# Three quarters of a down projection by seven block products, and constant products while the first tokens load

## The chip, the cores and the metric

The kernel runs on one core of a Trainium2 chip. Its engines are TensorE (PE, matrix products; PEld is its loading of the stationary operand), VectorE (DVE), ScalarE (ACT), GpSimd (POOL) and SyncE (SP); each works its own queue in order and waits for the others by semaphores. The metric is the time of one execution on the device in microseconds; less is better.

## What is computed

A decoder of two layers over 512 tokens of width 1024: differential attention, then latent attention, each followed by a feed-forward part with a squared ReLU, and a last normalization. The change lies in the feed-forward part of the second layer and at the very start.

```python
def sq_relu_mlp(hn, w_up, w_down):
    return jnp.square(jax.nn.relu(hn @ w_up)) @ w_down
...
            h = h + mla_attention(hn, w_dq[j], q_norm_g[j], w_uq[j], w_o_b[j],
                                  k_nope, k_rope, v, cos_b, sin_b)
        h = h + sq_relu_mlp(rms_norm(h, mlp_norm_g[l]), w_up[l], w_down[l])
    return rms_norm(h, final_norm_g)
```

`w_up` is 1024 x 4096, `w_down` 4096 x 1024, everything in float32.

## The kernel before

Products are made in a type of 32 bits that TensorE takes in one pass (`F32R`). To keep precision each operand is split in a high part (a cast on ScalarE) and a low part (a subtraction on VectorE), and a product is a triple, `mm3` (line 343): high by high, high by low, low by high, each with 128 x 128 stationary and up to 512 moving columns. A k-tile is 128 of the summed dimension, a token tile 128 tokens.

`Weights` (`W`, line 60) streams the weights. A unit of up to 1152 columns is loaded to one of 4 raw buffers (`load`, DMAs on SP's queue), cast (`prep_h`, L101) and subtracted (`prep`, L113) into one of 3 pairs of buffers. `get` takes the next unit, and `ahead` prepares the one behind it while TensorE works on the taken one.

The last feed-forward part goes in two halves of 2048 hidden features. `hidden` (line 672) makes 16 k-tiles of hidden features of all 512 tokens, two per job: 16 triples with the weights stationary and the normalized residual moving. Its `done` takes the ReLU on ScalarE (L676), multiplies it by the product on VectorE (L677: the square), and splits the result (L332, L333). `down_tokens` (line 813) then has the hidden tiles stationary and 512 columns of the down projection moving: for each of the two column halves (`fc`) it sums 16 k-tiles for four token tiles in four PSUM banks, and `token_done` adds them, scaled, to the residual rows `rtok`. Four such passes are made: 4 x 16 x 4 = 256 triples. The last one closes token by token: square and sum on ScalarE, a reciprocal root on GpSimd, two scalings and two output DMAs, whose place in the order of ScalarE's and VectorE's queues is set by due times (`OUT_US`, `later`). `side` (line 215) puts the turning of the residual into token rows (`scale1`) between the triples of the first up projection.

At the start, the identity, the gains and the tokens are loaded. `gain_cols` turns the gains into columns (`gcol`) on TensorE; a DMA that reads `gcol` (`held`) holds back the further loads on SP's queue. Per token tile `turn_x` makes eight transposes, multiplies by the gains on VectorE, splits, and copies the residual; value products fill TensorE between. `sum_x` then squares and sums each token half on ScalarE, and the reciprocal roots follow on GpSimd (`rsqrt_cols`).

A planner fixes the order in each engine's queue when the program is built; it may take an instruction ahead of others written before it, except in stretches in which the written order is kept (`nc.kept`: the start and the last pass).

Of the kernel before, what the change touches and what calls it, by code (L numbers as in the profile page):

```python
# [15 lines left out]
P = 128  # L16
T = 512
# [42 lines left out]
class Weights:  # L60
# [5 lines left out]
    def __init__(self, nc, pool, size):  # L66
        self.nc, self.pool, self.size = nc, pool, size
        self.specs, self.raws, self.parts = [], [], []
        self.taken = self.split = 0
        self.eng = nc.vector  # L70

    def add(self, name, shape, loads, beside=False, outs=None, eng=None):

# [10 lines left out]
    def load(self, upto, queue=None):  # L84
        while len(self.raws) < min(upto, len(self.specs)):
            name, shape, loads, *_ = self.specs[len(self.raws)]
            raw = self.tile(F32, name + "r", "raw", shape, self.RAW)
# [4 lines left out]
    def prep_h(self, upto):  # L92

        while len(self.parts) < min(upto, len(self.specs)):
            n = len(self.parts)
            self.load(n + 1)
            name, shape, _, beside, outs, eng = self.specs[n]
# [6 lines left out]
    def prep(self, upto):  # L104

        self.prep_h(upto)
        while self.split < min(upto, len(self.specs)):
# [8 lines left out]
            self.load(n + 1 + self.RAW)  # L116
# [8 lines left out]
    def ahead(self):  # L125
        self.prep(self.taken + 1)
# [103 lines left out]
OUT_US = (2.3, 2.6)  # L230
ROPE_US = (7, 9.0)
AT_TABLES = 3.5
# [29 lines left out]
def trunk(ctx: ExitStack, tc: tile.TileContext, io: dict, out: bass.AP):  # L262
# [80 lines left out]
    def mm3(dst, a, b, start, stop):  # L343

        (ah, al), (bh, bl) = a, b
        nc.tensor.matmul(dst, ah, bh, start=start, stop=False)  # L346
        nc.tensor.matmul(dst, ah, bl, start=False, stop=False)  # L347
        nc.tensor.matmul(dst, al, bh, start=False, stop=stop)  # L348
# [457 lines left out]
    hid1 = [[], []]  # L806
# [6 lines left out]
    def down_tokens(w_dn, hid, half, fc, last):  # L813

        units = [(w_unit(w_dn, fc * T, T, 16 * half + k, 2, f"m1d{half}{fc}_{k}"), k) for k in range(0, 16, 2)]
        tags = ("s", "s", "tr", "tr") if (half + fc) % 2 else ("acc", "acc", "acc", "o")
        late = 2 if last else 0

        def job():
            dsts = [bank(f"m1d{half}{fc}{i}", t) for i, t in enumerate(tags)]  # L820

            def mul(i, w, k):
                for kk in range(2):
                    yield mm3(dsts[i], sub(hid[k + kk], ALL, slice(i * P, (i + 1) * P)), sub(w, ALL, kk),
                              k + kk == 0, k + kk == 15)

            for u, k in units[:8 - late]:
                w = W.get(u)
                for i in range(NT):
# [3 lines left out]
                    if k == 14:  # L833
                        token_done(i, dsts[i], half, fc)
            ws = [(W.get(u), k) for u, k in units[8 - late:]]
            for i in range(NT if late else 0):
                for w, k in ws:
                    yield from mul(i, w, k)
                token_done(i, dsts[i], half, fc)
        return 16 * NT * 3 * PASS * T, job  # L840

    def token_done(i, dst, half, fc):
        t = rtok[i][fc]
        nc.vector.scalar_tensor_tensor(t, dst, r2c[:, i:i + 1], t, op0=ALU.mult, op1=ALU.add)
        if half == 0:
            return
        junk = big("fjunk")
        nc.scalar.activation(junk, t, AF.Square, accum_out=fss[:, i, fc:fc + 1])
        if fc == 0:
            nc.gpsimd.tensor_mul(t, t, gfin[0][:, :T])  # L850
# [11 lines left out]
        def out_second():  # L862
            nc.vector.scalar_tensor_tensor(t, t, f, gfin[0][:, T:], op0=ALU.mult, op1=ALU.mult)
# [301 lines left out]
```

## Time and profile before

| | us |
|---|---|
| median of 3 runs (lowest, highest) | 1147.07 (1147.04, 1147.47) |
| the profiled execution, its own time | 1147.38 |
| its span, first to last instruction | 1145.6 |
| TensorE busy | 1125.5 (98%) |
| VectorE busy | 649.5 (57%) |
| ScalarE busy | 496.9 (43%) |

A busy share is time in which an instruction of the engine was under way. Ends of matrix products are modelled, and products overlap, so the pace of TensorE is read from the distance of starts. A group is named by its line, the tile it writes and those it reads; L51 stands for all instructions in stretches of kept order, whatever line wrote them. Behind a group's times stands the idle time of its engine just before it, with what ended it.

### The profile page before, as it was taken

To read this page: it belongs to the slowest core of one execution; us is meant where nothing else is said; L and a number is where in the kernel's file an instruction comes from. 1 tells how busy PE (TensorE), PEld (TensorE's weight loads), DVE (VectorE), ACT (ScalarE), POOL (GpSimd) and SP (SyncE) were. 2 spreads that over 40 slices of the span, in tenths; PEclk is the share of its full clock that TensorE was granted. 3 is DMA by queue.
4 is the path that set the end of the run, shared out by engine and by line. 5 is a ranking of instruction groups with operands and counts; after the bars stand their busy time and mean duration, and the time that the engine had idled before them with its cause. 6 is when DMAs were issued, how large, how long until landed. Compare 5 with 4: busy or idle time off the path is not lost.

```text
span 1145.6 us, 14137 instructions
## 1 busy us (share of the span) xinstructions
PE 1125.5 (98%) x5528; PEld 945.5 (83%) x5528; DVE 649.5 (57%) x1148; ACT 496.9 (43%) x910; POOL 70.6 (6%) x63
## 2 busy tenths in 40 slices
PE   7999999999999999999999999999999999999996
PEld 7778998878888888888888889988888888888885
DVE  5898989876443234444455898855444223444232
ACT  6567666654341213443334666534433112343132
POOL 1000000030000010000111000013000000000011
PEclk9999999999999999999999999999999999999998
DMA  7321222123233333332332220123322333333211
GB/s 230 103 71 56 74 75 75 55 74 111 92 94 108 93 92 93 108 94 92 93 100 80 78 74 19 56 92 92 92 92 92 99 103 92 92 101 101 92 55 74
DMA packets 98321, 102.06 MB, mean 89 GB/s; under 512 B 4896, under 2 KB 86478, under 8 KB 98254
## 3 DMA queue, kind: packets, MB, share of 16 engines
q1 hardware_dynamic: 96974, 99.51, 28.2%
q10 hardware_dynamic: 1280, 1.65, 0.4%
q8 instruction: 43, 0.70, 0.2%
q14 instruction: 24, 0.20, 0.1%
HBM read 99.05 MB, written 2.10 MB: 88 GB/s over the span
## 4 chain that ended last, share of the span: by engine, by line
PE 79%; DVE 12%; ACT 4%; issue 2%; DMA 1%; SPq 1%; POOL 1%; ACTq 0%; POOLq 0%; DVEq 0%
PE m0d L346 5%; PE m1u L346 5%; PE m0d L348 5%; PE m1u L348 5%; PE m0u L347 5%; PE m0u L346 5%; PE m0d L347 5%; PE m1u L347 5%; PE m0u L348 5%; PE m1d L347 4%; PE m1d L348 4%; PE m1d L346 4%; PE m1d L51 3%; PE ob L346 1%; PE ob L348 1%
## 5 line engine op out<-in xcount | busy, mean ns | idle before, releaser
L346 PE MATMUL m1u<-xn1h,m1u_4h 128*128 128x512 f32 x128 | 50.3, 393 | 0.0
L346 PE MATMUL m1u<-xn0h,m1u_0h 128*128 128x512 f32 x128 | 50.2, 392 | 0.0
L348 PE MATMUL m1u<-xn1h,m1u_4l 128*128 128x512 f32 x128 | 49.9, 390 | 0.0
L348 PE MATMUL m1u<-xn0h,m1u_0l 128*128 128x512 f32 x128 | 49.9, 390 | 0.0
L347 PE MATMUL m1u<-xn1l,m1u_4h 128*128 128x512 f32 x128 | 49.8, 389 | 0.0
L347 PE MATMUL m1u<-xn0l,m1u_0h 128*128 128x512 f32 x128 | 49.8, 389 | 0.0
L347 PE MATMUL m0u<-xm0l,m0u_0h 128*128 128x512 f32 x128 | 49.8, 389 | 0.0
L346 PE MATMUL m0u<-xm0h,m0u_0h 128*128 128x512 f32 x128 | 49.8, 389 | 0.0
L346 PE MATMUL m0u<-xm1h,m0u_4h 128*128 128x512 f32 x128 | 49.8, 389 | 0.0
L347 PE MATMUL m0u<-xm1l,m0u_4h 128*128 128x512 f32 x128 | 49.8, 389 | 0.0
L348 PE MATMUL m0u<-xm0h,m0u_0l 128*128 128x512 f32 x128 | 49.8, 389 | 0.0
L348 PE MATMUL m0u<-xm1h,m0u_4l 128*128 128x512 f32 x128 | 49.8, 389 | 0.0
L113 DVE TENSOR_TENSOR m1u_4l<-m1u_4r,m1u_4h 128x1024 fp32r<-128x1024 f32 x16 | 19.6, 1225 | 36.5 <-ACT m1u_4h L101 36.5
L113 DVE TENSOR_TENSOR m0u_4l<-m0u_4r,m0u_4h 128x1024 fp32r<-128x1024 f32 x16 | 19.9, 1245 | 33.4 <-ACT m0u_4h L101 33.2
L677 DVE TENSOR_TENSOR m1a<-m1u,m1a 128x512 f32<-128x512 f32 x32 | 22.0, 687 | 21.7 <-ACT m1a L676 21.7
L677 DVE TENSOR_TENSOR m0a<-m0u,m0a 128x512 f32<-128x512 f32 x32 | 21.9, 686 | 19.4 <-ACT m0a L676 19.4
L101 ACT CAST m1u_4h<-m1u_4r 128x1024 fp32r<-128x1024 f32 x16 | 16.8, 1052 | 34.7 <-PE m1u L347 21.6
L676 ACT ACTIVATE m0a<-m0u 128x512 f32<-128x512 f32 x32 | 18.9, 592 | 29.4 <-PE m0u L348 29.4
L676 ACT ACTIVATE m1a<-m1u 128x512 f32<-128x512 f32 x32 | 19.0, 592 | 27.6 <-PE m1u L348 27.6
L101 ACT CAST m0u_4h<-m0u_4r 128x1024 fp32r<-128x1024 f32 x16 | 16.8, 1052 | 31.7 <-PE m0u L347 25.5
L363 POOL TENSOR_TENSOR ssq_m<-ssq_m,sq 128x512 f32<-128x512 f32 x14 | 21.3, 1519 | 149.8 <-ACT sq L362 149.7
L113 DVE TENSOR_TENSOR m0u_0l<-m0u_0r,m0u_0h 128x1024 fp32r<-128x1024 f32 x16 | 21.0, 1310 | 14.7 <-ACT m0u_0h L101 14.4
(2306 smaller groups left out, 3522.9 us busy)
## 6 DMA issues: line engine op xcount, KB each, us to landing
m0u_0r<-in_w_up SPq DMA_DIRECT2D x16, 512.0 KB, 3.7
m0u_4r<-in_w_up SPq DMA_DIRECT2D x16, 512.0 KB, 3.6
m1u_0r<-in_w_up SPq DMA_DIRECT2D x16, 512.0 KB, 3.6
m1u_4r<-in_w_up SPq DMA_DIRECT2D x16, 512.0 KB, 3.7
wq_0r<-in_w_qkv_a SPq DMA_DIRECT2D x8, 512.0 KB, 3.9
wk_0r<-in_w_qkv_a SPq DMA_DIRECT2D x8, 512.0 KB, 5.0
xt<-in_x SPq DMA_DIRECT2D x8, 256.0 KB, 4.8
wv_0r<-in_w_qkv_a SPq DMA_DIRECT2D x4, 512.0 KB, 3.5
```

The lines of the kernel that those rows point to most:

```text
L51: return self.owner.tc.keep_in_program_order(op(*args, **kw))
L101: self.nc.scalar.copy(d(h), v(self.raws[n]))
L113: eng.tensor_sub(d(to), v(self.raws[n]), d(h).bitcast(F32))
L346: nc.tensor.matmul(dst, ah, bh, start=start, stop=False)
L347: nc.tensor.matmul(dst, ah, bl, start=False, stop=False)
L348: nc.tensor.matmul(dst, al, bh, start=False, stop=stop)
L363: eng(nc).tensor_add(accum, accum, sq)
L676: nc.scalar.activation(a, dst, AF.Relu)
L677: nc.vector.tensor_mul(a, dst, a)
```

## The change

Chunks 0 to 2 of 8 k-tiles each (24 of the 32) of the last down projection go by Winograd's form of Strassen's scheme: hidden features A (512 tokens x 1024) and weights B (1024 x 1024) of a chunk are cut in 2 x 2 blocks, and seven products of blocks, or of sums of blocks, take the place of eight. `ORDER` names them with the chain of PSUM banks that each is added to and the quarter of the result that the chain is then added to. The last 8 k-tiles go by `down_tokens`, now with 8 k-tiles in each pass.

The sums of hidden blocks (S1 to S4) and of weight blocks (T1 to T4) are made on VectorE in full precision, and each of the seven operands on either side is then split: `pair` for A, units of `W` for B, with the raw block in place of a load. `hidden_tile` squares on ScalarE, 256 tokens at a time, straight into the A blocks. The up projection of the next chunk is cut in half jobs (4 of the 8 k-tiles for both features) that stand between the block products: product (P), half job (U), and so on, seven of each and an eighth half job. `steps` says what is started with each. `W` is now prepared two units ahead in this stretch. The raw blocks of B lie in buffers of the attention and in the residual's, which has been turned by then.

At the start 18 products of a constant with itself stand ahead of the first transposes and 14 more behind them; the gains are turned behind the first token tile's transposes; `held` reads the identity; four of the eight square sums go to VectorE. At the end the second last token's first scaling has a later due time, and the final gains lie in two tiles.

```diff
...
                 eng.tensor_sub(d(to), v(self.raws[n]), d(h).bitcast(F32))
...
-            self.load(n + 1 + self.RAW)
+            k, ahead = n + 1, 0
+            while k < len(self.specs) and ahead < self.RAW:
+                ahead += not callable(self.specs[k][2])
+                k += 1
+            self.load(k)
...
     def ahead(self):
-        self.prep(self.taken + 1)
+        self.prep(self.taken + self.lead)
...
 SPACE = 0.5
-OUT_US = (2.3, 2.6)
+OUT_US = (2.3, 2.6, 3.0)
 ROPE_US = (7, 9.0)
+WARM = (18, 14)
...
+    class Sevenths:
+        ORDER = (("A11", "B11", "u", [(0, 0)]), ("A12", "B21", "v", [(0, 0)]), ("S2", "T2", "u", [(0, 1)]),
+                 ("S1", "T1", "w", [(1, 1)]), ("S3", "T3", "u", [(1, 1)]), ("S4", "B22", "w", [(0, 1)]),
+                 ("A22", "T4", "u", [(1, 0)]))
+        made = 0
...
+        def hidden_tile(self, n, a):
+            k, u, j = n // 4, n % 4 // 2, n % 2
+            for m in range(2):
+                name = f"A{m + 1}{k + 1}"
+                if j == 0:
+                    self.a.setdefault(name, []).append(big(f"m1{name}{self.at}{u}").rearrange("p (k q) -> p k q", k=2))
+                nc.scalar.activation(self.a[name][u][:, j, :], a[:, m * 256:(m + 1) * 256], AF.Square)
+        def load_b(self, *names):
+            for name in names:
+                k, n = int(name[1]) - 1, int(name[2]) - 1
+                if n == 0:
+                    self.b[name] = [ap.tile([P, 2, T], F32, name=f"m1{name}{self.at}{u}", tag=("ath", "atl")[k], bufs=2)
+                                    for u in range(2)]
+                else:
+                    self.b[name] = [res[:, 4 * k + 2 * u:4 * k + 2 * u + 2, :] for u in range(2)]
+                for u in range(2):
+                    nc.sync.dma_start(self.b[name][u], w_view(self.w_dn, n * T, T, 8 * self.at + 4 * k + 2 * u, 2))
...
+        def sum_a(self, to, x, y, op, place=None):
+            x, y = self.a[x], self.a[y]
+            t = self.a[place] if place else [big(f"m1{to}{self.at}{u}").rearrange("p (k q) -> p k q", k=2) for u in range(2)]
+            for u in range(2):
+                nc.vector.tensor_tensor(t[u], x[u], y[u], op)
+            self.a[to] = t
+        def sum_b(self, to, x, y, place=None):
...
+        def pair(self, name):
+            spare = key_rests[2 * (Sevenths.made % 2):][:2]
+            Sevenths.made += 1
+            self.pairs[name] = [split(a.rearrange("p k q -> p (k q)"), name, tiles=spare[u])
+                                for u, a in enumerate(self.a[name])]
...
+        def product(self, i, units):
+            a, b, chain, to = self.ORDER[i]
+            first = chain not in self.banks
+            if first:
+                self.banks[chain] = [bank(f"m1{chain}{self.at}{t}", "s" if chain == "u" else "tr") for t in range(2)]
+            for u in range(2):
+                w = W.get(units[u])
+                for t in range(2):
+                    for j in range(2):
+                        tok = slice(j * 256 + t * P, j * 256 + (t + 1) * P)
+                        yield mm3(self.banks[chain][t], sub(self.pairs[a][u], ALL, tok), sub(w, ALL, j),
+                                  first and u == j == 0, u == j == 1, skip_group_check=True)
+                        if t == j == 0:
+                            W.ahead()
+                    if u == 1:
+                        for m, n in to:
+                            x = rtok[2 * m + t][n]
+                            tok = 2 * m + t
+                            nc.vector.scalar_tensor_tensor(x, self.banks[chain][t], r2c[:, tok:tok + 1], x,
+                                                           op0=ALU.mult, op1=ALU.add)
...
-        later.add(OUT_US[0], out_first)
+        later.add(OUT_US[2 if i == NT - 2 else 0], out_first)
         later.add(OUT_US[1], out_second)
...
+    CHUNKS = 3
+    sevenths = [Sevenths(c, io["w_down"][1]) for c in range(CHUNKS)]
...
+    def hidden_half(mp, half):
...
+        def done(m, dst):
+            c, n = mp // 4, 2 * (mp % 4) + m
+            a = big("m1a")
+            nc.scalar.activation(a, dst, AF.Relu)
+            if c < CHUNKS:
+                sevenths[c].hidden_tile(n, a)
+            else:
+                nc.vector.tensor_mul(a, dst, a)
+                hid1.append(split(a, "m1h"))
...
+    def seven(c):
...
+        steps = {
+            ("P", 0): lambda: (s.pair("A12"), s.sum_b("T1", "B12", "B11"), s.sum_a("S1", "A21", "A22", ALU.add)),
+            ("U", 0): lambda: (s.sum_b("T2", "B22", "T1"), load("B11")),
+            ("P", 1): lambda: (s.sum_a("S2", "S1", "A11", ALU.subtract), s.pair("S2")),
+            ("U", 1): lambda: s.sum_b("T3", "B22", "B12", "B12"),
+            ("P", 2): lambda: (s.pair("S1"), s.sum_a("S4", "A12", "S2", ALU.subtract, "A12")),
+            ("U", 2): lambda: (s.sum_b("T4", "B21", "T2", "T2"), load("B21")),
+            ("P", 3): lambda: (s.sum_a("S3", "A11", "A21", ALU.subtract, "A21"), s.pair("S3")),
+            ("P", 4): lambda: s.pair("S4"),
+            ("P", 5): lambda: (s.pair("A22"), load("B12")),
+            ("P", 6): lambda: (load("B22"), nxt is not None and nxt.pair("A11")),
+        }
...
+        def job():
+            for i in range(7):
+                yield from with_step(("P", i), s.product(i, plan[i]))
+                yield from with_step(("U", i), halves[i]())
+            yield from halves[7]()
+        return (7 * 8 + 8 * 16 / 2) * 3 * PASS * T, job
+    up1 = [hidden_half(mp, h) for mp in range(4) for h in range(2)]
+    both1 = [seven(c) for c in range(CHUNKS)]
+    down1 = [down_tokens(io["w_down"][1], hid1, fc, fc == 1) for fc in range(2)]
...
-        nc.sync.dma_start(held, gcol[0:1, 0:1])
+        nc.sync.dma_start(held, ident[0:1, 0:1])
...
-    gain_cols(grow_attn, 16, G_ATTN_A)
     more_loads()
+    def warm(n, name):
+        dst = bank(name, "o")
+        for _ in range(n):
+            nc.tensor.matmul(dst[:, :P], ones, ones, start=True, stop=True)
+    warm(WARM[0], "warm0")
...
+        if i == 0:
+            gain_cols(grow_attn, 16, G_ATTN_A)
+            warm(WARM[1], "warm1")
...
-            nc.scalar.activation(junk, xt[i][n], AF.Square, accum_out=ss0[:, 2 * i + n:2 * i + n + 1])
+            ss = ss0[:, 2 * i + n:2 * i + n + 1]
+            if n:
+                nc.vector.tensor_tensor_reduce(junk, xt[i][n], xt[i][n], 1.0, 0.0, ALU.mult, ALU.add, ss)
+            else:
+                nc.scalar.activation(junk, xt[i][n], AF.Square, accum_out=ss)
...
-    side(up1[0], scale1(), 4.0)
-    gfin.append(ap.tile([P, D], F32, name="gfin", tag="atl", bufs=2))
-    nc.sync.dma_start(gfin[0], io["final_norm_g"].rearrange("(o d) -> o d", o=1).broadcast_to([P, D]))
-    Filler(down1[0] + up1[1] + down1[1][:1]).drain()
+    sevenths[0].load_b("B11", "B21")
+    side([(16 * 3 * PASS * T / 2, job) for job in up1[:6]], scale1(), 2.0)
+    sevenths[0].load_b("B12", "B22")
+    sevenths[0].pair("A11")
+    Filler([(16 * 3 * PASS * T / 2, job) for job in up1[6:]]).drain()
+    W.lead = 2
+    Filler(both1).drain()
+    W.lead = 1
+    gfin += [big(f"gfin{n}") for n in range(2)]
+    for n in range(2):
+        nc.sync.dma_start(gfin[n], io["final_norm_g"][n * T:(n + 1) * T].rearrange("(o d) -> o d", o=1).broadcast_to([P, T]))
+    Filler(down1[:1]).drain()
     nc.kept = True
-    Filler(down1[1][1:]).drain()
+    Filler(down1[1:]).drain()
...
```

## Rows read from the trace of the kernel before

**Rows 1.** The page's first part: busy us (share of the span) and instructions.
```profile
PE 1125.5 (98%) x5528; PEld 945.5 (83%) x5528; DVE 649.5 (57%) x1148; ACT 496.9 (43%) x910; POOL 70.6 (6%) x63
```

**Rows 2.** The waits of TensorE: in total us, times, longest; three of eleven.
```profile
PE gps L51 <- DMA grow_attn<-in_attn_norm_g: 4.7, 1, 4.7
PE va0vps L51 <- ACT wv_0h L51: 1.2, 1, 1.2
PE rb_ps L321 <- POOL r L51: 1.1, 1, 1.1
...
```

**Rows 3.** Busy time by stretch: PE, PEld, DVE, ACT, POOL, then clock, DMA share, GB/s.
```profile
60.00:80.00 20.00, 19.25 (x96) 15.63 (x95) 19.76 (x50) 13.87 (x30) 0.00 (x0) 1.00 0.27 79
240.00:260.00 20.00, 20.00 (x90) 16.57 (x89) 17.24 (x18) 12.08 (x18) 10.15 (x7) 1.00 0.35 105
...
910.00:1136.00 226.00, 226.00 (x993) 186.07 (x992) 82.10 (x95) 66.01 (x87) 6.89 (x7) 1.00 0.27 88
```

**Rows 4.** Timeline (start, us, what), the last 72 products: the first and the last.
```profile
1119.63 0.39 PE L51 MATMUL m1d<-m1d_10h,m1hh 128*128 128x512 f32 x1
...
1135.72 0.39 PE L51 MATMUL m1d<-m1d_14h,m1hl 128*128 128x512 f32 x1
```

**Rows 5.** Groups of instructions, 786 to 1136 us: busy us, mean ns, idle before them.
```profile
L677 DVE TENSOR_TENSOR m1a<-m1u,m1a 128x512 f32<-128x512 f32 x32 | 22.0, 687 | 21.7 <-ACT m1a L676 21.7
...
L113 DVE TENSOR_TENSOR m1u_4l<-m1u_4r,m1u_4h 128x1024 fp32r<-128x1024 f32 x15 | 18.4, 1225 | 36.3 <-ACT m1u_4h L101 36.3
...
L333 DVE TENSOR_TENSOR m1hl<-m1a,m1hh 128x512 fp32r<-128x512 f32 x24 | 16.6, 692 | 16.6 <-ACT m1hh L332 16.6
L101 ACT CAST m1u_4h<-m1u_4r 128x1024 fp32r<-128x1024 f32 x15 | 15.8, 1052 | 34.2 <-PE m1u L347 21.6 <-issue 8.2 <-PE m1d L348 4.4
```

**Rows 6.** Timeline of the end.
```profile
1136.35 0.74 DVE L51 SCALAR_TENSOR_TENSOR rt<-m1d,r2c,rt 128x512 f32<-128x512 f32 x1
...
1138.00 0.63 ACT L51 ACTIVATE fjunk<-rt 128x512 f32<-128x512 f32 x1 [0.41 <-ACT rt L51]
```

**Rows 7.** Timeline of the square sums, 24 to 32 us.
```profile
24.67 1.27 ACT L101 CAST wk_0h<-wk_0r 128x1024 fp32r<-128x1024 f32 x1
...
25.98 1.26 DVE L113 TENSOR_TENSOR wk_0l<-wk_0r,wk_0h 128x1024 fp32r<-128x1024 f32 x1 [1.90 <-ACT wk_0h L101]
...
28.91 0.62 ACT L51 ACTIVATE junk<-xt 128x512 f32<-128x512 f32 x1
...
29.65 0.63 ACT L51 ACTIVATE junk<-xt 128x512 f32<-128x512 f32 x1
...
31.61 0.43 PE L321 MATMUL rb_ps<-ident,r 128*128 128x128 f32 x2 [1.05 <-POOL r L51]
```

**Rows 8.** Timeline of the first 15 us; xT are a token tile's transposes.
```profile
4.90 1.97 PE L51 MATMUL xT<-ident,xt 128*128 128x128 f32 x8
...
5.01 0.17 ACT L51 COPY gcol<-gps 128x16 f32<-128x16 f32 x1 [1.85 <-PE gps L51]
...
6.13 1.47 DVE L51 TENSOR_TENSOR x<-xT,gcol 128x512 f32<-128x512 f32 x2 [5.11 <-PE xT L51]
...
8.86 0.58 PE L51 MATMUL va0vps<-wv_0l,xa0h 128*128 128x256 f32 x1 [0.23 <-DVE wv_0l L51]
...
11.37 1.91 PE L51 MATMUL xT<-ident,xt 128*128 128x128 f32 x8
...
12.46 0.69 DVE L51 TENSOR_TENSOR x<-xT,gcol 128x512 f32<-128x512 f32 x1 [1.25 <-PE xT L51]
...
13.31 0.69 DVE L51 TENSOR_TENSOR x<-xT,gcol 128x512 f32<-128x512 f32 x1 [0.16 <-PE xT L51]
...
15.00 1.03 PE L51 MATMUL xT<-ident,xt 128*128 128x128 f32 x8
```

**Rows 9.** Timeline: two neighbouring products of 128 columns in the attention.
```profile
48.41 0.27 PE L479 MATMUL a0s<-k0d,q0s 128*128 128x128 f32 x1
...
48.52 0.27 PE L480 MATMUL a0s<-krest,q0s 128*128 128x128 f32 x1
```

## What I predict

> **What bounds the kernel now.** I read four views, in this order. The page's first part shows TensorE busy for 98% of the span, VectorE for 57% [rows 1]. A busy share of TensorE is modelled, so the next view is its waits: the largest is 4.7 us before the first product, the next two, of 1.2 and 1.1, also lie in the first 32 us, and none of the list lies in the last layer's feed-forward part [rows 2]. The busy times by stretch then show that part (910 to 1136 us): 993 products recorded in 226 us, VectorE busy for 82.1 of them, so 36% [rows 3]. Last, the timeline of the end: 72 products start between 1119.63 and 1135.72, hence 16.09 / 71 = 0.2266 us from start to start [rows 4]; the 226 us by their count give 0.2276, with a few records missing. This stage is bound by TensorE alone, and each product taken out of it is worth 0.2266 us, as long as the operands of the next one are there.
>
> **Part 1: seven block products.** The last down projection has 32 k-tiles x 4 token tiles x 2 halves = 256 triples (mm3), each of three products. Three chunks of 8 k-tiles now take 7 block products of 8 triples, 56 in place of 64. So 3 x 8 x 3 = 72 products go: 72 x 0.2266 = **16.3 us**, all on the path [rows 4]. The up projection keeps its 256 triples; it is only cut in half jobs and put between the block products. A chunk is 7 x 8 + 8 x 8 = 120 triples = 360 products = 81.6 us.
>
> What pays for this is VectorE. Per chunk: 22 weight units are split (14 for the block products, 8 of the up projection). Of these 16 are single subtractions of 1024 columns at 1.225 us, 19.6; the six of T1, T2 and T4 are two of 512 each, 12 x 0.692 = 8.3. The sums T: 12 of 512 and 2 of 1024, 8.3 + 2.5 = 10.8. The sums S: 8 x 0.692 = 5.5. Seven pairs of A blocks: 14 subtractions, 9.7 [rows 5]. Results into the token rows: 14 x 0.74 = 10.4 [rows 6]. Together **64.3 us of 81.6, 79%**. In the third chunk the up projection makes the ordinary hidden tiles of the last quarter: 8 x (0.687 + 0.692) = 11.0 more and 1.4 less for a pair that no next chunk needs, 73.9 us, **91%** [rows 5]. ScalarE, with half of 1.05 us for each 512 columns or fewer, has 22 x 1.05 + 14 x 0.53 + 24 x 0.53 = 43 us, 53%, and isn't the bound [rows 5].
>
> Does TensorE stay fed at such shares? The trace has both sides. From 240 to 260 us VectorE is busy for 17.24 of 20 us (86%) and TensorE starts 90 products, its full pace. From 60 to 80 us VectorE is busy for 19.76 of 20 (99%) and TensorE is idle for 0.75 us, 4% [rows 3]. By the first, the first two chunks cost nothing; by the second, the third costs up to 0.04 x 81.6 = 3.3 us, and all three 10. The load is not even: the first slot of a chunk (product, half job) has 13.5 us of VectorE work in 10.9 us, the second 10.7 (13.4 in the third chunk), the third 11.0, the other four 29 us in 49. But T1, T2 and T3 need only loaded blocks, which land in the slots before, and this planner does pull work forward: the cast at 24.67 us (L101) was written behind all eight square sums (L51), and runs between them [rows 7]. There is one tight place per chunk: the unit of the first half job can be cast only when a weight buffer comes free, as the chunk begins, and must be split 5.4 us later; 1.05 + 1.225 of it is its own, and up to 3 us of casts and sums can stand ahead. I take **2.0 us** of stalls in all, nearer the 86% row, since two chunks of three lie below it; bounds 0 and 10.
>
> Waits added: the first chain is added to again (product 3 of 7) after VectorE has read its banks behind product 1, with three jobs of 5.4 us between; the loads of the next chunk's blocks stand in SP's queue behind the sums that read the old ones, and hold the loads of up-projection weights behind them, which are four units of 10.9 us ahead. Both cost nothing with that cover; without it each is a wait of the 1.5 us of two results or of one load. The bytes loaded are the same. The transposes of the residual only come closer together.
>
> **Part 2: the start.** Before, the first token tile's eight transposes take 1.97 us at 4.90; the third tile's take 1.03 at 15.00 [rows 8]. [...] Now 18 constant products start once the constant is written, about 1.2 us. A product of 128 columns of this type takes 0.11 us from start to start at the high level [rows 9]; times 1.97 / 1.03 it is 0.21 at the low one (an estimate), so they end at about 5.0 us, when the first transposes are due.
> [...]
>
> Whether the clock is up by then, rows can't tell, so both ends. The gain columns, ready at 5.18 before (copy at 5.01), are now made behind the eight transposes: 0.5 us after their end. High clock: transposes end at 6.0, VectorE's first multiply (6.13 before) starts at 6.5, 0.4 late. Low clock: 7.0 and 7.5, 1.3 late. From there VectorE is busy without a pause to 11.2 (12.46 less 1.25), so it ends that at 11.6 or 12.5; the second tile's second multiply, at 13.31 before because its transposes ran at the low level (11.37, 1.91 us), then starts at 12.3 or 13.2. Gain 1.0 or 0.1 [rows 8]; I take 0.6. The loads behind the held one start about half a microsecond sooner, which covers that.
> Four of eight square sums move to VectorE: ScalarE spends 0.74 us from one to the next [rows 7], so the last is done some 3 us sooner, and the 1.05 us that TensorE waits at 31.61 for the reciprocal roots made from them goes. VectorE takes them in its pauses (1.90 us before 25.98) [rows 7]. Head together **1.6 us**, bounds -0.5 (low clock, and the second set of constant products in the way) and 2.5.
>
> **Part 3: the end.** The last token's square (1138.00) stands behind the scaling of the token before and its output's issue on ScalarE's queue, though its input, begun at 1136.35, is there at 1137.1 [rows 6]. A due time of 3.0 in place of 2.3 puts it ahead, since a token takes 2.6. Everything behind moves up 0.86 us; but four output transfers then lie closer together. I take **0.6 us**, bounds 0 and 0.9. Half-size final gains move work off no path.
>
> **The sum**, against the profiled execution (1147.38: span 1145.6 and 1.8 around it): 1147.38 - 16.3 + 2.0 - 1.6 - 0.6 = 1130.9. That execution is 0.3 above the median of the runs, so 1130.6.
>
> **Rivals.** A: VectorE does bound the stage in places. Its first three slots per chunk are full or over, and its queue is worked in order; if nothing is pulled forward, the first half job of each chunk waits for four passes of ScalarE over the last hidden tile (2.1), the last subtraction of A12 (0.7), T1 (2.8), S1 (1.4) and its own split (1.2), 8.2 us against 5.4, so 2.8 per chunk, and the third chunk's second slot adds 2.5: 10.9, 8.9 more than my 2: **1139.5**. For it: 91% in the third chunk. Against: the 240 to 260 us row [rows 3].
> B, the other side: VectorE stands idle before every weight split until ScalarE's cast is done, with the sums queued behind it. That is 22 x 1.05 = 23 us per chunk on top of 64.3 or 73.9: 87.4, 87.4 and 97.0 against 81.6, 27 us in all, 25 more than my 2: **1156**. The three chunks have 42 us to spare and the change 18.5 us to lose, so it decides from a pause of 60.8 / 66 = 0.92 us before each split. For it: in the stage now VectorE idles 36 us before 15 such splits [rows 5]. Against: it idles there for want of work; at 60 to 80 us the same splits leave it 0.24 us of 20 [rows 3].
> [...]
> C: the constant products miss, with the head 0.5 slower and the wait at 31.61 merely moved: 1130.6 + 2.1 = **1132.7**.
>
> **How the numbers follow.** Forecast 0.68 (1127.5 to 1135 by its own bounds: head and end at their best with no stall, or 6 us of stalls), A 0.20, C 0.07, B 0.05. The range 1127.3 to 1139.5 holds the forecast, C and half of A. A difference under 0.2% (2.3 us) can't be told from none here. Faster by more: the forecast, A and C, less its worst tail, 0.93; within: 0.02; slower: 0.05.
>
> **What would show it.** Right: 72 fewer products in the feed-forward part, their spacing still 0.227 us, VectorE near 80, 80 and 91% in three stretches of some 82 us, waits of TensorE there of 2 us in sum; no wait at 31.6; the last square right behind its token's sum. Wrong: gaps of TensorE at the first half job of a chunk, released by a weight's low part (A), or at every unit (B); transposes of the first tile still at 1.97 us and the first multiply past 7.4 (C).

## The result, and the profile after

| | us |
|---|---|
| before, median of 4 runs (lowest, highest) | 1147.27 (1147.04, 1147.8) |
| after, median of 4 runs | 1133.84 (1133.03, 1134.65) |
| ratio, 95% interval | 0.9882 (0.987, 0.9895) |
| the profiled execution of after, its span | 1133.83, 1132.0 |

The change gains 13.4 us. The forecast was 1130.6: the time lies in its range and 3.2 above its centre. The page of after, first part (busy us, share of the span, instructions), answers to [rows 1]:

```profile
PE 1118.1 (99%) x5488; PEld 938.6 (83%) x5488; DVE 731.7 (65%) x1286; ACT 539.1 (48%) x1004; POOL 71.0 (6%) x63
```

VectorE took over 82 us of work, ScalarE 42, and TensorE is still busy throughout. Its waits in after, the four largest (total us, times, longest), beside [rows 2]:

```profile
PE m1csps L381 <- POOL ssq_m L375: 1.3, 1, 1.3
PE warm L51 <- DVE ones L51: 1.1, 1, 1.1
PE rb_ps L333 <- POOL r L51: 0.9, 1, 0.9
PE a7rb_ps L333 <- POOL a7r L605: 0.9, 1, 0.9
```

Two of these speak against the forecast: the wait for the reciprocal roots (`rb_ps`) is still there, and one of 1.3 us on GpSimd (`m1csps`), the largest, is new. None lies in the three chunks. Their stretches (TensorE, weight loads, VectorE, ScalarE, GpSimd busy, then clock, DMA share, GB/s), beside [rows 3]:

```profile
786.00:838.00 52.00, 51.72 (x246) 42.78 (x247) 16.76 (x22) 26.10 (x46) 1.25 (x2) 1.00 0.36 121
838.00:920.00 82.00, 82.00 (x357) 66.88 (x357) 57.98 (x78) 41.01 (x66) 0.00 (x0) 1.00 0.32 103
920.00:1002.00 82.00, 82.00 (x358) 66.88 (x357) 57.99 (x78) 41.23 (x66) 0.00 (x0) 1.00 0.28 90
1002.00:1084.00 82.00, 82.00 (x357) 66.79 (x356) 63.74 (x85) 36.69 (x53) 0.00 (x0) 1.00 0.20 65
```

VectorE is busy for 58, 58 and 63.7 of 82 us: 71, 71 and 78%, not 79, 79 and 91. TensorE never idles there, and yet it starts 357 products in 82 us, where a spacing of 0.2266 us would give 362. So something in the products themselves is slower.

The start of after (start, us, engine, what; in brackets the idle time before it and what ended it), beside [rows 8] and [rows 7]:

```profile
1.08 4.10 PE L51 MATMUL warm<-ones 128*128 128x128 f32 x18 [1.08 <-DVE ones L51]
4.98 1.93 PE L51 MATMUL xT<-ident,xt 128*128 128x128 f32 x8
7.16 0.17 ACT L51 COPY gcol<-gps 128x16 f32<-128x16 f32 x1 [4.00 <-PE gps L51]
7.36 1.29 DVE L51 TENSOR_TENSOR x<-xT,gcol 128x512 f32<-128x512 f32 x2 [6.34 <-ACT gcol L51]
7.38 3.25 PE L51 MATMUL warm<-ones 128*128 128x128 f32 x14 [0.26 <-ACT gcol L51]
10.43 0.52 PE L51 MATMUL va0vps<-wv_0h,xa0h 128*128 128x256 f32 x1
...
29.58 0.15 DVE L51 TENSOR_TENSOR ms<-ss 128x2 f32<-128x2 f32 x1
...
32.34 0.43 PE L333 MATMUL rb_ps<-ident,r 128*128 128x128 f32 x2 [0.94 <-POOL r L51]
```

The clock records of the packed trace begin at 14.10 us, with 1.00 (at 13.36 in before). Ahead of that TensorE goes at a slower pace: value products of 256 columns start 0.21 us apart from 10.75 to 12.88 and 0.12 apart from 14.58 on, and a tile's transposes take 1.93 us at 4.98 and 1.04 at 16.54. These two paces are called the low and the high level of the clock here, and the begin of its records its rise; the clock column of the stretches shows 1.00 ahead of the rise too.

The end of after, beside [rows 4] and [rows 6]:

```profile
1124.17 0.39 PE L51 MATMUL m1d<-m1d_6h,m1hl 128*128 128x512 f32 x1
1124.81 0.74 DVE L51 SCALAR_TENSOR_TENSOR rt<-m1d,r2c,rt 128x512 f32<-128x512 f32 x1
1125.58 0.63 ACT L51 ACTIVATE fjunk<-rt 128x512 f32<-128x512 f32 x1 [1.60 <-DVE rt L51]
1128.40 0.37 ACTq L968 DMA_DIRECT2D out<-rt  x1
```

**Where the time went**, by three marks in both traces: the first product of the last up projection, the last product, the end of the span.

| stretch | before | after | measured | forecast |
|---|---|---|---|---|
| start to the first product of the last up projection | 781.46 | 782.12 | +0.65 | -1.6 |
| from there to the last product | 354.26 | 342.05 | -12.2 | -14.3 |
| last product to the end | 9.84 | 7.87 | -2.0 | -0.6 |
| sum | | | -13.52 | -16.5 |

So three terms were off, two against the forecast and one for it. My theory after this reading: the block products gain their 16.3 us less a price on each of them, which comes from where `krest` lies in memory; the first stage is slowed by constant products of 128 columns, with which the clock rose no sooner than at 14.1 us; the new wait comes from `side`. The rivals: the products are slower because VectorE and ScalarE load the memory more, or the start is worth something all the same and the loss lies elsewhere.

### The profile page after: what moved, and what is told of

Its sections match the earlier page's. It is cut to its first block, busy times and chain, and to the rows that moved or that the text cites. A ratio compares the mean times of both kernels' runs of the same rounds, so it can differ in the third digit from the quotient of the medians.

```text
span 1132.0 us, 14312 instructions
## 1 busy us (share of the span) xinstructions
PE 1118.1 (99%) x5488; PEld 938.6 (83%) x5488; DVE 731.7 (65%) x1286; ACT 539.1 (48%) x1004; POOL 71.0 (6%) x63
## 4 chain that ended last, share of the span: by engine, by line
PE 78%; DVE 12%; ACT 4%; issue 2%; DMA 1%; POOL 1%; SPq 1%; ACTq 0%; POOLq 0%; DVEq 0%
PE m1u L358 7%; PE m1u L360 7%; PE m1u L359 7%; PE m0d L358 5%; PE m0d L360 5%; PE m0u L359 5%; PE m0d L359 5%; PE m0u L358 5%; PE m0u L360 5%; PE ob L358 1%; PE ob L359 1%; PE ob L360 1%; PE m1d L51 1%; PE m1w L359 1%; PE m1w L358 1%
## 5 line engine op out<-in xcount | busy, mean ns | idle before, releaser
L358 PE MATMUL m1u<-xn1h,m1u_1h 128*128 128x512 f32 x128 | 50.3, 393 | 0.0
L360 PE MATMUL m1u<-xn1h,m1u_1l 128*128 128x512 f32 x128 | 50.0, 390 | 0.0
L359 PE MATMUL m1u<-xn1l,m1u_1h 128*128 128x512 f32 x128 | 49.9, 390 | 0.0
L120 DVE TENSOR_TENSOR m1u_0l<-m1u_0r,m1u_0h 128x1024 fp32r<-128x1024 f32 x16 | 19.6, 1223 | 27.0 <-ACT m1u_0h L108 27.0
L345 DVE TENSOR_TENSOR krest<-m1A,krest 128x512 fp32r<-128x512 f32 x30 | 20.7, 689 | 21.1 <-ACT krest L344 20.8
L120 DVE TENSOR_TENSOR m1u_1l<-m1u_1r,m1u_1h 128x1024 fp32r<-128x1024 f32 x16 | 19.6, 1224 | 22.1 <-ACT m1u_1h L108 22.1
L108 ACT CAST m1u_1h<-m1u_1r 128x1024 fp32r<-128x1024 f32 x16 | 16.8, 1051 | 33.7 <-PE m1u L359 23.6
L344 ACT CAST krest<-m1A 128x512 fp32r<-128x512 f32 x30 | 18.4, 617 | 26.1 <-PE m1w L359 11.5
```

The source lines that it names most:

```text
L108: self.nc.scalar.copy(d(h), v(self.raws[n]))
L120: eng.tensor_sub(d(to), v(self.raws[n]), d(h).bitcast(F32))
L344: nc.scalar.copy(h, src)
L345: nc.vector.tensor_sub(l, src, h.bitcast(F32))
L358: nc.tensor.matmul(dst, ah, bh, start=start, stop=False, **kw)
L359: nc.tensor.matmul(dst, ah, bl, start=False, stop=False, **kw)
```

## The experiments

Each is the changed kernel with one edit (the twelfth: the kernel before). The kernel before, run beside them, had medians of 1147.05 (e1 to e4), 1147.15 (e5, e6, e7, e9) and 1147.46 us (e8, e10 to e12). Intervals of a ratio are about 0.0015 to either side, so of differences near 1.5 us the traces decide.

### The products' own pace: where krest lies

`krest` holds the split A blocks, stationary in all 504 block products, and, earlier in the kernel, some of the attention's keys and hidden tiles of the first layer, which are the moving operand there. As the program is laid out, it begins at a multiple of 128 bytes in each partition, while the weight buffers that it is multiplied with, and the other hidden tiles and the normalized residuals, begin 64 bytes behind one. The trace of before already had such products. Groups of instructions of before, 786 to 1136 us (busy us, mean ns, idle before them): two of the down projection, the first with `krest` stationary, the second without.

```profile
L347 PE MATMUL m1d<-m1d_0l,krest 128*128 128x512 f32 x24 | 9.5, 396 | 0.0
...
L347 PE MATMUL m1d<-m1d_6l,m1hh 128*128 128x512 f32 x24 | 9.3, 389 | 0.0
```

7 ns more for each of the first kind. In after all block products are of that kind. Timeline of after, the first product of a block of 24 and of the next job:

```profile
865.18 0.40 PE L358 MATMUL m1w<-m1T100h,krest 128*128 128x512 f32 x1
...
870.78 0.39 PE L358 MATMUL m1u<-xn1h,m1u_1h 128*128 128x512 f32 x1
```

5.60 us for 24 products: 0.2333 each. **e3** moves `krest` by 64 bytes, and what follows it by 64 more.

```diff
+    const.tile([P, 16], F32, name="pad0")
     key_rests = [[const.tile([P, T], F32R, name=f"krest{n}{c}") for c in range(2)] for n in range(KEY_RESTS)]
+    const.tile([P, 16], F32, name="pad1")
```

> The changed kernel with 64 bytes of nothing ahead of the krest tiles and 64 behind them, so that these tiles begin 64 bytes further (64 past a multiple of 128 in place of 0) and every other operand keeps its place by 128. Theory 1, the block products start every 0.2333 us in place of 0.2266 because their stationary operand lies at another offset by 128 bytes than the moving one: the 504 block products fall to about 0.227, 3 us in all, and the 310 products that have a krest tile as moving operand from 0.2303 to 0.227, 1 us: 1130 us. Theory 2, it is the place of these tiles at the low end of the memory, or the short runs of one product: spacing and time stay, 1133.8 us.

Measured: 1128.65 us (1127.99 to 1131.02), ratio 0.9843 (0.9828, 0.9857), 5.2 less than after. The same block in e3:

```profile
862.69 0.39 PE L358 MATMUL m1w<-m1T100h,krest 128*128 128x512 f32 x1
...
868.13 0.39 PE L358 MATMUL m1u<-xn1h,m1u_1h 128*128 128x512 f32 x1
```

and its first chunk's stretch:

```profile
838.00:920.00 82.00, 82.00 (x363) 67.95 (x362) 59.23 (x80) 41.25 (x66) 0.00 (x0) 1.00 0.33 105
```

5.44 us for 24, so 0.2267, and 363 products in 82 us in place of 357, with VectorE and ScalarE as busy as before the edit. The load of the other engines isn't the cause. That leaves two readings: an address at a multiple of 128 is slow by itself, or two operands that differ in it are. **e9** tells them apart: a pad behind `krest` alone brings those other operands to a multiple of 128 too.

```diff
     key_rests = [[const.tile([P, T], F32R, name=f"krest{n}{c}") for c in range(2)] for n in range(KEY_RESTS)]
+    const.tile([P, 16], F32, name="pad1")
```

> The changed kernel with 64 bytes of nothing behind the krest tiles only, so that they stay at multiples of 128 bytes and every other operand of the products comes to one too. Theory 1, a product is slow when its two operands begin at different offsets by 128 bytes: the block products fall to 0.227 us, as with the krest tiles moved, and all others stay, 1129 us. Theory 2, an operand at a multiple of 128 bytes is slow by itself: all products go to 0.230 to 0.233, and the kernel is over 15 us slower.

Measured: 1128.52 us (1128.07 to 1130.72), ratio 0.9842 (0.9827, 0.9856); the block products at 0.2267, and no group slower than in e3. So it is the difference of the two operands, not the place of one. Only a difference of 64 bytes and none were tried; that 128 is the period isn't shown. **e12** is the edit of e3 on the kernel before, which has 192 products with `krest` stationary.

> The kernel before with krest shifted by 64 bytes; nothing else differs. It has 192 products with krest stationary and 340 with it moving, against 504 and 340 in the changed kernel. By the spacings (0.2335 against 0.2266 stationary, 0.2296 against 0.2267 moving) it takes 1.3 + 1.0 = 2.3 us less than the kernel before, 1144.8; then the change alone, with all operands aligned, is worth 1144.8 - 1128.6 = 16.2 us. If the shift acts in another way than through these products, its gain here isn't 2.3 but 5.2 as in the changed kernel (1142) or nothing (1147.1).

Measured: 1144.83 us (1144.41 to 1145.78), ratio 0.9978 (0.9969, 0.9987), 2.6 less than its 1147.46. So the change brought 2.6 us of this cost with it (5.2 less 2.6), and with the operands alike in both kernels it is worth 1144.83 - 1128.65 = 16.2 us (15.8 if each is taken against the kernel before that ran beside it: 18.4 less 2.6).

### The new wait

**e4** gives `side`, which puts the turning of the residual between the triples of the first up projection, its old spacing.

```diff
-    side([(16 * 3 * PASS * T / 2, job) for job in up1[:6]], scale1(), 2.0)
+    side([(16 * 3 * PASS * T / 2, job) for job in up1[:6]], scale1(), 4.0)
```

> The changed kernel with 4.0 us of products, as before, in place of 2.0 between the steps that turn the residual into token rows. Theory 1, the wait of 1.28 us on GpSimd ahead of the column sums is the price of their earlier place: it goes, 1132.5 us. Theory 2, it is hidden by what follows: 1133.8 us.

Measured: 1131.98 us (1131.56 to 1132.68), ratio 0.9869 (0.9854, 0.9883), 1.9 less. The sums over the partitions (`m1csps`) that stand ahead of the turning read `ssq_m`, which GpSimd adds up. Timeline of after, then of e4:

```profile
784.47 1.76 POOL L375 TENSOR_TENSOR ssq_m<-ssq_m,sq 128x512 f32<-128x512 f32 x1 [1.46 <-ACT sq L374]
786.28 1.05 PE L381 MATMUL m1csps<-ones,ssq_m 128*128 128x2 f32 x8 [1.28 <-POOL ssq_m L375]
```
```profile
783.92 1.78 POOL L375 TENSOR_TENSOR ssq_m<-ssq_m,sq 128x512 f32<-128x512 f32 x1 [1.46 <-ACT sq L374]
786.33 0.95 PE L381 MATMUL m1csps<-ones,ssq_m 128*128 128x2 f32 x8
```

With 2.0 the sums come up in TensorE's queue 1.28 us before GpSimd is done, and all products stand behind them; with 4.0 products fill that time. In some executions the pause costs more. In three of the nine profiled kernels that have it, the granted clock (third number from the end) fell behind it, as in e2's from 784 to 790 us:

```profile
784.00:790.00 6.00, 4.71 (x20) 3.69 (x19) 1.89 (x5) 0.62 (x2) 2.77 (x2) 0.78 0.28 87
```

The records of before and after have two values, 1.00 and, behind the last product, 0.50. In e2, e6 and e8 the clock fell from 787 or 788 on for 3.4 us if it stood at 0.50 (means of 0.78 from 784 to 790 and 0.90 from 790 to 794 in e2), which loses 1.7 us of products by that count (from the first product of the last up projection to the last product they take 343.63 to 343.67 us, after 342.05); in the profiled execution of after it stood at 1.00 throughout, and in the three kernels without the wait as well. The wait need not be the only place: of the executions of e10 and e11, which lack it, one each has a mean granted clock of 0.996, the others 0.998 or 0.999, and those two took 1126.91 and 1126.82 us; they weren't profiled.

### The start

**e1** has the whole old start: no constants, the gains first, `held` on the gain columns, all square sums on ScalarE.

```diff
-WARM = (18, 14)
+WARM = (0, 0)
...
-        nc.sync.dma_start(held, ident[0:1, 0:1])
+        nc.sync.dma_start(held, gcol[0:1, 0:1])
...
+    gain_cols(grow_attn, 16, G_ATTN_A)
     more_loads()
...
-            gain_cols(grow_attn, 16, G_ATTN_A)
...
-            if n:
+            if False:
```

> The changed kernel with the whole start of the kernel before: no constant products, gains turned ahead of the first transposes, held read from the gains, all eight square sums on ScalarE. If the new start gains the 1.6 us that I predicted, this kernel is 1.6 slower than the changed one, some 1135.4 us. If it costs what its trace shows (the first product of the last up projection starts 0.65 us later than in the kernel before), it is 0.65 faster, some 1133.2, and the first value product is back at 8.05 us.

Measured: 1133.73 us (1133.31 to 1134.38), ratio 0.9884 (0.9868, 0.9901): the same as after. The first value product is back at 8.04 us (10.43 in after), and the clock rises at 14.44 (14.10). The new start is worth nothing that these runs can tell. **e2** takes out the constant products alone.

```diff
-WARM = (18, 14)
+WARM = (0, 0)
```

> The changed kernel without its 18 and 14 constant products; the rest of the new start stays. Theory 1, the constant products hold up the value products (10.43 us in place of 9.2, when their operands are ready) and don't lift the clock: the first value product comes at about 9.2 us and the kernel is 0.5 to 1.2 us faster. Theory 2, they lift the clock as meant: the clock's rise comes later than 13.9 us here, and the kernel is 0.5 to 1.5 us slower.

Measured: 1134.62 us (1133.53 to 1135.67), ratio 0.9891 (0.9876, 0.9906). The clock rises at 15.99 here, and at 12.45 to 14.10 in the seven traces with these constants (after, e3, e4, e6 to e9), so they may bring it forward; but the three traces with the old start, which has none, have 13.36 to 14.44 (before, e12, e1). Against that the first set holds the transposes (they start at 4.14 here, at 4.98 in after), and the second the value products (9.52 and 10.43). The time is within 1 us of after's, less than the intervals tell apart. **e5** makes the constant products 512 columns wide, 9 and 7 of them, and leaves the rest of the start.

```diff
-WARM = (18, 14)
+WARM = (9, 7)
...
-            nc.tensor.matmul(dst[:, :P], ones, ones, start=True, stop=True)
+            nc.tensor.matmul(dst, ones, ones[:, 0:1].to_broadcast([P, T]), start=True, stop=True)
```

> The changed kernel with 9 and 7 constant products of 512 columns in place of 18 and 14 of 128 (the moving operand is one column of the constant, read 512 times), about the same time at the low level, 0.43 us each. In the runs so far the granted clock rose between 12.4 and 16.0 us, whether or not 18 constant products ran from 1.1 to 5.2 us. Theory 1, products of 128 columns leave the array too idle to lift the clock: the rise comes before 9 us here, the first tile's transposes or the first value products run at the high level, and the time falls by about 1 us. Theory 2, constant products don't lift it at all: the rise stays between 12.4 and 16 us and the time is that of the changed kernel within 1 us.

Measured: 1131.63 us (1131.15 to 1133.18), ratio 0.9867 (0.9852, 0.9882), 2.2 less; the first product of the last up projection at 779.92, 2.2 sooner than in after and 1.5 sooner than before. That is outside the spread of the five traces that have the narrow constants and `krest` in its place (after, e4, e6, e7, e8: 781.38 to 782.12), and with `krest` moved it comes again: 778.11 and 778.24 in e10 and e11, 780.19 and 780.29 in e3 and e9. Timeline of e5:

```profile
1.08 4.21 PE L51 MATMUL warm<-ones 128*128 128x512 f32 x9 [1.08 <-DVE ones L51]
5.08 1.61 PE L51 MATMUL xT<-ident,xt 128*128 128x128 f32 x8
...
7.12 1.79 PE L51 MATMUL warm<-ones 128*128 128x512 f32 x7 [0.26 <-ACT gcol L51]
...
11.23 1.03 PE L51 MATMUL xT<-ident,xt 128*128 128x128 f32 x8
```

The first set of constants fills TensorE for about the same time as in after (4.21 and 4.10 us), but here the clock rises at 6.26 us, within the first tile's transposes, and the second tile's transposes take 1.03 us, which is the higher level [rows 8].

### VectorE's reserve

**e6** adds two operations without use (a minimum of a tile with itself, 128 x 512) to VectorE at the head of each block product, 42 in all; **e7** adds four, 84.

```diff
                 if at == 0 and name in steps:
                     steps[name]()
+                if at == 0 and name[0] == 'P':
+                    for _ in range(2):
+                        nc.vector.tensor_tensor(idle[0], idle[0], idle[0], ALU.min)
```

> The changed kernel with two idle minima of 512 columns on VectorE (0.62 us each from start to start) ahead of each of the 21 block products: VectorE goes from 58, 58 and 64 us to 67, 67 and 73 of 82, about the load that I had costed. Theory 1, my step was right and only the load was over-sized: stalls of some 2 us appear. Theory 2, the planner keeps TensorE fed at 89% too: no wait of TensorE in these stretches and 1133.8 us.

> The same with four idle minima ahead of each block product: VectorE at 75, 75 and 81 us of 82. If its queue is what bounds the block products at last, TensorE waits here, by 2 us a chunk at 92% and 4 at 99%: some 1142 us. If VectorE can be filled to 92% without a wait, only the third chunk waits: 1135 to 1137 us.

Measured: e6 1134.07 us (1133.99 to 1134.71), ratio 0.9887 (0.9873, 0.9902); e7 1135.92 (1135.0 to 1136.16), ratio 0.9903 (0.9886, 0.9919). Neither loaded the chunks evenly: the planner drew the added operations forward, all of e6's to 787 to 826 us, ahead of the first chunk, where VectorE had been busy for a quarter of the time (9.9 of 40 us), and e7's to 787 to 914 us. So e6 tests nothing. In e7 the first chunk and the stretch ahead of it (48.6 of 52 us) had the load; the chunk's stretch, and its one wait:

```profile
838.00:920.00 82.00, 80.87 (x351) 65.69 (x351) 79.09 (x111) 40.68 (x66) 0.00 (x0) 1.00 0.34 107
```
```profile
PE m1u L360 <- DVE m1u_0l L120: 1.1, 1, 1.1
```

At 79.1 of 82 us, 96%, TensorE waits once, 1.1 us, for the low part of a half job's weights; the wait ends at 839.82, at the head of the chunk, and none follows. That is the place rival A named, at a load the change doesn't reach. Loads between 78% and this weren't tried.

### The end

**e8** gives the second last token's first scaling its old due time.

```diff
-        later.add(OUT_US[2 if i == NT - 2 else 0], out_first)
+        later.add(OUT_US[0], out_first)
```

> The changed kernel with the old due time (2.3) for the second last token's first scaling; nothing else differs. The last product to the end of the span took 9.84 us before and 7.87 after. If the due time brought only the 0.86 us by which the last output is issued sooner, this takes 1134.7, and the rest of the 2.0 us belongs to the half-size final gains or to the outputs' transfers; if it brought all of it, 1135.8; if the transfers lying closer together give it back, 1133.8.

Measured: 1135.73 us (1134.84 to 1136.14), ratio 0.9897 (0.9883, 0.991). The time is 1.9 above after's, but the profiled execution is one of the three whose clock fell, so its marks are better evidence: 5.10 us from the last product to the last issue on ScalarE's queue (5.09 before, 4.23 after), and 3.77 from that issue to the end (4.75 before, 3.63 after). Timeline of e8, the square that waits and the last issue:

```profile
1126.64 0.72 ACT L51 ACTIVATE rt<-rt,fr 128x512 f32<-128x512 f32 x1 [1.34 <-POOL fr L51]
1127.39 0.34 ACTq L968 DMA_DIRECT2D out<-rt  x1
1127.78 0.63 ACT L51 ACTIVATE fjunk<-rt 128x512 f32<-128x512 f32 x1 [0.41 <-ACT rt L51]
...
1130.59 0.37 ACTq L968 DMA_DIRECT2D out<-rt  x1
```

So the due time brings 0.87 us, and 0.14 at most behind the issue. The other 1.0 us of the end's gain is there with the old due time too, behind the last issue, where only the transfers of the outputs run. e12, with the final gains in one tile as before, has 4.75 again. The list of DMA packets has a difference there. In before, 1138 to 1150 us (packets, MB, share of 16 engines):

```profile
q14 instruction: 1, 0.01, 0.2%
```

By the trace's packet records this packet of 8 KB, whose queue is of the kind `instruction`, runs 7.03 to 7.34 us after the last product's start, among the last packets of the outputs, of which the last six then follow one another until 8.25. e12 has the same (7.05 to 7.35, and 8.27). e8 has no such packet there, and its outputs end at 7.49; nor has any trace of the changed kernel or of its other variants behind the last product. So 0.8 of the 1.0 us goes with that packet. No run moves it alone, and none has the half-size gains alone.

### The three together

**e10** has the edits of e3, e4 and e5; **e11** has them with the gains turned ahead of the first transposes, and 5 constants behind these.

> The changed kernel with three edits that were measured alone: krest shifted by 64 bytes (-5.2), the residual's turning every 4.0 again (-1.9), constant products of 512 columns, 9 and 7 (-2.2). If the three are separate costs of TensorE's own path, they add: 1124.5, between 1124 and 1125.5. If the wide constants' gain and that of the wait on the square sums are partly one and the same (a pause after which the clock falls in some executions), the sum is up to 1.7 less: 1126.2.

> As the combined kernel (krest shifted, turning every 4.0, wide constants), but with the gains turned ahead of the first transposes again and 5 constant products behind the transposes in place of 7. The copy of the gain columns ends at 7.3 us after, and at 5.2 before; the multiply behind it could start at once when the transposes end, some 0.5 us sooner. If VectorE's chain sets the head, 0.5 us less than the combined kernel; if TensorE's queue or the landing of the tokens sets it, the same; if the gains, which land at 4.7, hold the transposes back, up to 0.3 more.

Measured: e10 1125.4 us (1124.37 to 1126.91), ratio 0.9811 (0.9798, 0.9824); e11 1125.16 (1124.5 to 1126.82), ratio 0.9808 (0.9795, 0.9821). The three costs add, to within 0.9 us: 8.4 less than the changed kernel, 22 less than the kernel before. The order of the gains makes no difference: with them first the copy ends at 5.96 and no longer holds VectorE, but the transposes start at 5.68, behind the wide constants and the gains, so the first multiply starts at 6.45, against 6.25 in e10.

## Why the prediction was right, and where it was off

**The 72 products: right.** From the first product of the last up projection to the last product, e10 and e11, with the operands alike and the new wait gone, take 336.61 us, and e12, the kernel before with the operands alike, 353.02: 16.4 less, where 16.3 was forecast. After, e1 and e5, which have the same products, agree there to 0.01 us. The change as it is has -12.2 in that stretch: -16.4 for the products, +1.5 for the new wait (342.05 in after, 340.52 in e4) and +2.7 for the offset of `krest` (3.9 from after to e3, less 1.2 from before to e12). That TensorE alone bounds the stage and that each product taken out is worth its spacing [rows 4] is borne out.

**The total: in part luck.** In the two profiled executions three terms cost more than I gave them (start 2.2, pace 2.7, new wait 1.5) and two less (stalls 2.0, end 1.4), so that only some 3 us of the misses are left in the total.

**Their pace: missed.** I took 0.2266 us from 72 products at the very end, whose stationary operand wasn't in `krest`, and priced all products by it. Block products took 0.2333. The grouped view of before had it, 396 against 389 ns, and I didn't read it: 2.6 us (2.7 by the marks). So had the 0.2276 of the whole stage [rows 3], which the prediction put down to missing records. No record is missing there (1576 products from the first of the last up projection on in before, 1504 in after, 72 fewer): 144 of the stretch's 993 products have `krest` stationary, and 144 x 0.0067 us is the difference.

**VectorE's stalls, 2.0: too much.** There is none. The instructions came out as counted, 78 in a chunk, but their durations overlap: operations of 0.68 to 0.74 us that follow each other without a pause start 0.60 to 0.66 apart (0.66 between 1124.15 and 1124.81 at the end of after). In the second chunk the durations add up to 62.7 us, and the busy time is 58, so a sum of durations came to 64.3. The third chunk's 91% was 78. And the planner does draw work forward, as e6 shows against what it was made for.

**The new wait: missed, 1.3 (1.5 by the marks).** I costed the closer spacing of `side` at nothing, since the transposes "only come closer together". What heads them is a sum that waits for GpSimd. The prediction named no cover for it; the cover was the products between, and the edit took them away. In the executions in which the clock fell behind the pause (e2, e6, e8) it cost 1.6 to 1.7 more.

**The start, -1.6: wrong, by 1.5 to 2.3.** The five traces of it lie -0.08 to +0.65 us from the one of before, so nothing was gained, and the +0.65 of the table is the worst of them. Each part of it had the low end of its bounds come true. The clock isn't up: the first transposes take 1.93 us, as before (1.97). The gains come late, and the first multiply starts at 7.36, as worked out for the low clock (7.5). The second set of constants writes the PSUM bank that the gain columns are copied from, so it starts only behind that copy and ends after the operands of the first value product are there; that product starts 2.4 us later than before. And the wait for the reciprocal roots stayed: the second sum was there at 29.58, but VectorE then took a weight's split of 1.27 us at 30.16, which the planner had drawn ahead, and only at 31.33 the one small operation that stands between the sum and GpSimd. Moving four squares off ScalarE only moved the place where it waits. The eighteen constants took 4.10 us, 0.22 from start to start, near the 0.21 estimated from the rows, and left no pause before the transposes.

**The end, -0.6: mis-sized, 2.0 measured.** The 0.86 us of the due time came as worked out, with no price behind it; 1.0 more came from behind the last issue, where the kernel before has a packet of a queue of the kind `instruction` among its last output packets; the prediction read no row of it.

**The rivals.** A fell: there is no wait in the chunks, and in e7 a load of 96% brings one, at the head of the chunk. B fell, though VectorE does stand idle for casts: for 24 of the 82 us in the first two chunks. Its two largest such groups in after, 920 to 1002 us (busy us, mean ns, idle before them and what ended it):

```profile
L345 DVE TENSOR_TENSOR krest<-m1A,krest 128x512 fp32r<-128x512 f32 x10 | 6.9, 689 | 7.4 <-ACT krest L344 7.3
L120 DVE TENSOR_TENSOR m1u_0l<-m1u_0r,m1u_0h 128x1024 fp32r<-128x1024 f32 x4 | 4.9, 1221 | 7.2 <-ACT m1u_0h L108 7.2
```

With 58 us of work that is no loss, and it isn't a fixed price per split: in e7 the added work fills these pauses, down to 2.9 us, and TensorE runs on. C came true as a mechanism: the constants missed and the wait at 31.61 only moved, to 32.34. Its 1132.7 is nearer to 1133.8 than the forecast; I gave it 0.07. What is left to it is the two costs that no case had, less the two that were better than thought.

## What to carry to other kernels

Price products by the group that the change will make more of, operand tiles included, not by the cleanest stretch of the trace: a few ns per product, times hundreds, were here a fifth of the gain. When work is moved closer together, look at what its first instruction waits for and which instructions covered that wait. And an edit whose gain hangs on a state that the trace of before doesn't show, here the clock under the constant products, is better priced at the bad end until one run shows the state.

## What was not expected of the hardware

- A product of 512 columns in this 32-bit type took 0.2267 us when both operands lay alike relative to 128 bytes (both at 0 in e9, both at 64 in e3), and 0.2333 when the stationary one lay 64 bytes off the moving one (after); with `krest` moving, 0.231 against 0.227 (medians, after and e3).
- Constant products of 128 columns kept TensorE at work from 1.08 to 6.9 us with the transposes, and the clock rose at 14.10 (12.45 to 14.10 in seven traces); with 512 columns it rose within such a stretch, at 6.26 (e5) and at 4.03 (e10).
- Behind one and the same pause of 1.3 us the granted clock fell in three profiled executions (means of 0.78, 0.79 and 0.86 from 784 to 790 us in e2, e6 and e8) and not in six (1.00).
- In both traces of the kernel before's end (before and e12) an 8 KB packet of a queue of the kind `instruction` ran among the last output packets, 7.03 to 7.35 us behind the last product's start, and these ended at 8.25 and 8.27 us, 0.8 later than in e8 (7.49), which has none there.
